# Modulation sums split around the low parts, their first product on ScalarE, and six loads moved to GpSimd's queue

## The chip, the cores and the metric

The program runs on one core of a Trainium2 chip. The metric is device time in microseconds (us), from the start of the program to its end on that core; lower is better. A core has TensorE (PE, matrix products), VectorE (DVE), ScalarE (ACT), GpSimd (POOL) and SyncE (SP, which here only issues transfers). Each runs its own list of instructions in order, and semaphores tie the lists together. Any of SP, GpSimd and ScalarE can issue a DMA; an instruction that waits holds back whatever stands behind it on its engine.

## The reference, cut to what matters

Two blocks are computed for 512 tokens of width 1024. The change touches the first alone:

```python
mod = silu(c) @ w_ada + b_ada              # c: 1 x 1024, w_ada: 1024 x 3072
shift, scale, gate = split(mod, 3)
h = x * (1 + scale) + shift                # 512 x 1024
p = h @ w_in
out_a = gmlp(p[..., :1536])                # u * v * silu(gate), v normed and mixed over tokens
out_b = rwkv7(p[..., 1536:])               # a recurrence over tokens, group norm, bonus, gate
o = concat([out_a, out_b]) @ w_out
x = layer_norm(ALPHA * x + gate * o)
```

The second block is latent attention with an MLP, and an HGRN2 mixer with an MLP.

## The kernel before

**Precision.** Every large product is made of three: an operand is split into a high part (`wh`, `aH`, a cast by ScalarE) and a low part (`wl`, `aL`, a subtraction by VectorE), and high×high, high×low and low×high are added in PSUM.

**The modulation** is the first 75 us. `w_ada`'s shift and scale columns come in four groups `g` of 256 columns each. For a group, VectorE forms the running sum `acc` = Σ over q of w_ada[q]·silu(c)[q] over eight 128-row pieces (128x512 numbers each): one tensor_scalar for q = 0 (line 343, shown by its helper's line as L127) and seven scalar_tensor_tensor (L132). TensorE then sums `acc` over the partitions with four products against ones, eight instructions in the trace (`sums`, "sm<-ones,acc"), and VectorE adds the bias: "mod". With mod, ScalarE turns the transposed x (`turned_x`, "sm<-ident,xt") into `h`, casts it to `aH`, and writes the residual `res`; VectorE makes `aL`. Tiles named "ada" hold w_ada (each half of a group, four pieces, is one tile of a ring of five), "raw" rows of w_in and other weights. A group loads 2 MB of w_ada and 0.5 MB of x, an iteration of the loop below 0.375 MB of w_in.

**The loop over k** = 0..7 multiplies h's eight slices of 128 columns by the rows of w_in, eighteen 512-column products each, group g = k // 2. In each iteration, after four of them (the constant SB = 1), TensorE transposes the x of k+1; in odd iterations the sums over the next group follow there. `part(g+1, 0)`, the first half of the next running sum, stands at the end of an even iteration, and `part(g+1, 1)`, the second half, in the next odd one, ahead of `sums`. The order of the code is the order on the engines here, held by a context (`ordered`).

**Later**, `out_gate` (lines 922 to 932) uses the same `ada_acc` for eight pieces of gate, 128x128 numbers a piece ("ga"). `ugate` (line 688) loads a finished tile of the gMLP branch's mix ("mx") back from DRAM and multiplies it by gelu(u) ("gsh") and the gate ("gt", "gbn"). `inverse` (lines 777 to 798) solves 32x32 triangular systems in 31 steps on VectorE with tiles XT, TV and a temporary, and passes the result through DRAM (scT) to `Tst` and `TTb`. `merge` (line 812) multiplies GpSimd's M by Tst on TensorE ("mg"), adds a unit matrix on VectorE ("Psb", L122) and multiplies by TTb: the first step of a chain over eight chunks. `post` (line 889) is the group norm of the chain's output, once per 128 tokens, with its scale and shift from DRAM (G2D, B2D, lines 909 and 911). While VectorE inverts, TensorE is fed with products of other branches. Here a scheduler orders instructions by priority, so that an edit can change places of its neighbours too.

Of the kernel before, what the change touches and what calls it, by code (L numbers as in the profile page):

```python
# [14 lines left out]
AF = mybir.ActivationFunctionType  # L15
# [5 lines left out]
P = 128  # L21
T = 512
# [9 lines left out]
FULL = slice(0, T)  # L32
LATE = (0, 0, 0, 0, 0, 2, 1, 0)
POSTS = (3, 4, 5, 7)
SB = 1
MB = 1
BEGUN = 1
TT = ("sm", "sm", "mm", "mm")
# [22 lines left out]
class Kern:  # L61
# [238 lines left out]
    def block1(self):  # L300
        nc, I, tc = self.nc, self.I, self.tc
# [10 lines left out]
        sc = b([P, 8], "sc")  # L312
# [7 lines left out]
        bonD, G2D, B2D, mixD, oaD = (dt_(n) for n in ("bonD", "G2D", "B2D", "mixD", "oaD"))  # L320
# [18 lines left out]
        def ada_acc(acc, raw, steps, q0=0):  # L339

            for q in steps:
                if q == 0:
                    self.ts(acc, raw[:, q - q0], sc[:, q : q + 1])
                else:
                    self.stt(acc, raw[:, q - q0], sc[:, q : q + 1], acc, ALU.mult, ALU.add)

# [31 lines left out]
        def part(g, cur, q):  # L378
            ada_acc(cur[2], cur[1][q], range(4 * q, 4 * q + 4), 4 * q)
# [25 lines left out]
        with self.ordered():  # L405
            self.petoken = "start"
            cur = load(0)
            rv = wrows(0)
            pt = turned_x(0, cur[0])
            part(0, cur, 0)  # L410
            part(0, cur, 1)
            sums(0, cur)
            w_ = self.wsplit(rv, 1, 6 * P)
            modulated(0, pt)
            for k in range(8):
                wh, wl = w_
                g = k // 2
                if k < 7:
                    rv = wrows(k + 1)
                if k % 2 == 0 and k < 6:  # L420
                    nxt = load(g + 1)
                for f in loads[3 * k : 3 * k + 3]:
                    f()
                tok = [slice(tb * P, (tb + 1) * P) for tb in range(NB)]
                for tb in range(NB):
                    self.mm(psv[tb], hH[k][:, tok[tb]], wh[:, 0, :T], k == 0, False)
                    self.mm(psv[tb], hH[k][:, tok[tb]], wl[:, 0, :T], False, False)
                    if tb == SB and k < 7:
                        pt = turned_x(k + 1, (nxt if k % 2 else cur)[0])
                        if k % 2:  # L430
                            part(g + 1, nxt, 1)
                            sums(g + 1, nxt)
                            cur = nxt
                        w_ = self.wsplit(rv, 1, 6 * P)
                        modulated(k + 1, pt)
                        if k % 2 == 0 and k < 6:
                            part(g + 1, nxt, 0)
                oz = ((T, psw), (T + P, psk))
                for o, pz in oz:
                    self.mm(pz, wh[:, 0, o : o + P], hH[k], k == 0, False)  # L440
                    self.mm(pz, wl[:, 0, o : o + P], hH[k], False, False)
                for tb in range(NB):
                    self.mm(psv[tb], hL[k][:, tok[tb]], wh[:, 0, :T], False, k == 7)
                for o, pz in oz:
                    self.mm(pz, wh[:, 0, o : o + P], hL[k], False, k == 7)
            self.petoken = None
            for k in range(8):
                self.st(nc.gpsimd.dma_start(out=xaD[k], in_=xa[k]))
# [237 lines left out]
            yield from part_gemm(w_in, 3072 + i * P, evac)  # L686

        def ugate(j, pool):
            mx = self.tl(pool, [P, T], "mx", bufs=1)
            nc.sync.dma_start(out=mx, in_=mixD[j])  # L690

            def u_evac(ps):
                ug = self.tl(pool, [P, T], "gsh", bufs=2)
                self.act(ug, ps, AF.Gelu_apprx_tanh)
                self.tt(mx, mx, ug, ALU.mult)

            def g_evac(ps):
                t = self.tl(pool, [P, T], "gt", bufs=2)
                self.act(t, ps, AF.Tanh, scale=0.5)
                x = self.tl(pool, [P, T], "gbn", bufs=1)  # L700
                self.copy(x, ps)
                self.stt(t, t, 1.0, x, ALU.add, ALU.mult)
                self.stt(t, mx, 0.5, t, ALU.mult, ALU.mult)
                nc.sync.dma_start(out=oaD[j], in_=t)

            yield from part_gemm(w_in, j * P, u_evac)
            yield from part_gemm(w_in, 1024 + j * P, g_evac)
# [12 lines left out]
        g = [prep(p) for p in range(4)]  # L720
# [44 lines left out]
        rp = rx_.enter_context(self.pool("rw", 1))  # L765
# [1 line left out]

        Xs = self.tl(rp, [P, 32, 32], "XT")
        Tm = self.tl(rp, [P, 32, 32], "TV")
        tmp = self.tl(rp, [P, T], "tmp", bufs=1)  # L770
        Bt = [r([P, 4, P], f"Bt{i}") for i in range(2)]
        Kt = [r([P, 4, P], f"Kt{i}") for i in range(2)]
        Tst = [r([P, 4, RC], f"Tst{i}") for i in range(2)]
# [118 lines left out]
        def post(tb):  # L892
# [13 lines left out]
            ts_ = slice(tb * P, (tb + 1) * P)  # L906
            yield
            g2 = self.tl(rp, [P, 4, P], "gsh", bufs=2)
            nc.sync.dma_start(out=g2, in_=G2D[:, :, ts_].rearrange("i p t -> p i t"))
            b2 = self.tl(rp, [P, 4, P], "gbn", bufs=1)  # L910
            nc.sync.dma_start(out=b2, in_=B2D[:, :, ts_].rearrange("i p t -> p i t"))
            ps = self.ptl("mg")
            for p in range(4):
                self.turn(ps[:, p * P : (p + 1) * P], yc.rearrange("p h i -> p (h i)")[:, p * P : (p + 1) * P])
# [909 lines left out]
```

## Time and profile before

| | us |
|---|---|
| median of three runs | 1630.25 (1630.16 to 1633.17) |
| the profiled execution's own time | 1626.63 |
| its span | 1624.5 |
| TensorE busy | 1546.4 (95%) |
| VectorE busy | 918.4 (57%) |
| ScalarE busy | 721.0 (44%) |
| GpSimd busy | 250.6 (15%) |
| mean granted clock of TensorE | 0.984 |

The span is what the trace covers; the execution's own time has 2.1 us more around it. A busy share is over the whole span; what an engine waits for is read from a stretch of it. In the rows, L127 is tensor_scalar, L132 scalar_tensor_tensor, L122 tensor_tensor, L136 an activation, L139 a copy or cast, L142 a matrix product, L148 a transpose: each is the helper that issues all of its kind, so rows are told apart by their tiles ("out<-in"). A granted clock of 1.00 is 2.4 GHz on TensorE, 0.50 is 1.2 GHz.

### The profile page before, as it was taken

To read this page: it belongs to the slowest core of one execution; us is meant where nothing else is said; L and a number is where in the kernel's file an instruction comes from. 1 tells how busy PE (TensorE), PEld (TensorE's weight loads), DVE (VectorE), ACT (ScalarE), POOL (GpSimd) and SP (SyncE) were. 2 spreads that over 40 slices of the span, in tenths; PEclk is the share of its full clock that TensorE was granted. 3 is DMA by queue.
4 is the path that set the end of the run, shared out by engine and by line. 5 is a ranking of instruction groups with operands and counts; after the bars stand their busy time and mean duration, and the time that the engine had idled before them with its cause. 6 is when DMAs were issued, how large, how long until landed. Compare 5 with 4: busy or idle time off the path is not lost. (4 is left out here: it accounts for less than half of the span.)

```text
span 1624.5 us, 21815 instructions
## 1 busy us (share of the span) xinstructions
PE 1546.4 (95%) x8309; PEld 1308.3 (81%) x8309; DVE 918.4 (57%) x1617; ACT 721.0 (44%) x1313; POOL 250.6 (15%) x406
## 2 busy tenths in 40 slices
PE   5899979989999999999999999999999999999997
PEld 4677768779978889888888897888888888888886
DVE  4568685667667838434343438667754824343445
ACT  3345425654655646333232335656745623322231
POOL 3120201214410013000000024223323200000000
PEclk9899999999999999999999999999999999999999
DMA  9533455543223122433333322322223223241421
GB/s 309 155 103 95 81 164 143 154 124 111 53 72 85 40 78 66 130 96 96 93 91 104 91 80 86 103 72 68 67 60 104 92 78 116 64 119 65 121 86 52
DMA packets 262091, 161.15 MB, mean 99 GB/s; under 512 B 29537, under 2 KB 242644, under 8 KB 261988
## 3 DMA queue, kind: packets, MB, share of 16 engines
q1 hardware_dynamic: 260260, 156.55, 33.4%
q0 software_dynamic: 1584, 2.97, 0.5%
q8 instruction: 65, 1.06, 0.3%
q14 instruction: 38, 0.31, 0.1%
q10 hardware_dynamic: 144, 0.26, 0.0%
HBM read 146.90 MB, written 11.53 MB: 98 GB/s over the span
## 5 line engine op out<-in xcount | busy, mean ns | idle before, releaser
L122 DVE TENSOR_TENSOR wl<-raw,wh 128x1024 fp32r<-128x1024 f32 (+3 forms) x244 | 286.8, 1177 | 307.8 <-ACT wh L139 303.6
L139 ACT CAST wh<-raw 128x1024 fp32r<-128x1024 f32 (+3 forms) x244 | 242.5, 996 | 468.6 <-PE mm L142 363.2
L142 PE MATMUL mm<-bL,wh 128*128 128x512 f32 (+1 forms) x752 | 281.3, 377 | 1.2 <-DVE bL L132 1.2
L142 PE MATMUL mm<-bH,wl 128*128 128x512 f32 (+1 forms) x752 | 280.6, 376 | 0.0
L142 PE MATMUL mm<-bH,wh 128*128 128x512 f32 (+1 forms) x752 | 278.4, 377 | 0.5 <-ACT t L136 0.4
L142 PE MATMUL mm<-aH,wh 128*128 128x512 f32 (+1 forms) x656 | 239.4, 366 | 6.6 <-DVE res L132 2.8
L142 PE MATMUL mm<-aH,wl 128*128 128x512 f32 (+1 forms) x656 | 236.9, 362 | 1.1 <-DVE wl L122 1.0
L142 PE MATMUL mm<-aL,wh 128*128 128x512 f32 (+1 forms) x656 | 237.1, 363 | 0.0
L142 PEld LDWEIGHTS mm<-bL,wh 128*128 128x128 f32 x752 | 140.7, 188 | 30.4 <-DVE bL L132 2.3
L142 PEld LDWEIGHTS mm<-bH,wl 128*128 128x128 f32 x752 | 140.7, 188 | 28.0
L142 PEld LDWEIGHTS mm<-bH,wh 128*128 128x128 f32 x752 | 138.7, 188 | 28.9 <-ACT t L136 0.8
L142 PEld LDWEIGHTS mm<-aH,wh 128*128 128x128 f32 x656 | 125.1, 191 | 27.5 <-issue 4.9
L142 PEld LDWEIGHTS mm<-aH,wl 128*128 128x128 f32 x656 | 125.2, 191 | 20.2 <-DVE wl L122 1.7
L142 PEld LDWEIGHTS mm<-aL,wh 128*128 128x128 f32 x656 | 125.5, 191 | 17.9 <-issue 0.2
L142 PE MATMUL mm<-wh,aH 128*128 128x512 f32 x288 | 114.8, 401 | 1.7 <-ACT aH L139 1.7
L142 PE MATMUL mm<-wl,aH 128*128 128x512 f32 x288 | 114.0, 398 | 0.0
L142 PE MATMUL mm<-wh,aL 128*128 128x512 f32 x288 | 109.1, 395 | 0.0
L139 ACT CAST aH<-t 128x512 fp32r<-128x512 f32 (+1 forms) x74 | 41.1, 563 | 75.6 <-DVE t L122 75.5
L142 PEld LDWEIGHTS mm<-wh,aH 128*128 128x128 f32 x288 | 55.3, 192 | 13.1 <-ACT aH L139 1.8
L122 DVE TENSOR_TENSOR aL<-t,aH 128x512 fp32r<-128x512 f32 (+1 forms) x74 | 45.1, 618 | 36.5 <-ACT aH L139 36.5
L142 PEld LDWEIGHTS mm<-wh,aL 128*128 128x128 f32 x288 | 55.3, 192 | 12.0
L142 PEld LDWEIGHTS mm<-wl,aH 128*128 128x128 f32 x288 | 55.4, 192 | 11.2
(548 smaller groups left out, 2622.4 us busy)
## 6 DMA issues: line engine op xcount, KB each, us to landing
raw<-in_mlp_w_dram SPq DMA_DIRECT2D x128, 512.0 KB
raw<-in_hgrn_w_in_dram SPq DMA_DIRECT2D x32, 512.0 KB
raw<-in_w_in_dram SPq DMA_DIRECT2D x23, 512.0 KB
ada<-in_w_ada_dram SPq DMA_DIRECT2D x16, 512.0 KB
raw<-in_w_out_dram SPq DMA_DIRECT2D x10, 512.0 KB
raw<-in_w_ada_dram SPq DMA_DIRECT2D x8, 512.0 KB
raw<-in_mla_w_o_dram SPq DMA_DIRECT2D x8, 512.0 KB
raw<-in_hgrn_w_o_dram SPq DMA_DIRECT2D x8, 512.0 KB
```

What stands on the lines that cost most here:

```text
L122: self.st((eng or self.nc.vector).tensor_tensor(out=out, in0=a, in1=b, op=op))
L139: self.st(self.nc.scalar.copy(out=out, in_=in_))
L142: i = self.nc.tensor.matmul(out, l, r, start=start, stop=stop, **kw)
```

## The change

1. `ada_acc`'s first product is an activation on ScalarE (Copy with a scale per partition) instead of VectorE's tensor_scalar: four times in the modulation (128x512), eight times in `out_gate` (128x128).
2. In the loop, `part(g+1, 0)` stands at the start of an even iteration, ahead of the split of k+1's weights and of `modulated(k+1)`, and `part(g+1, 1)` at its end. The transposes for k+1 (and in odd iterations the sums) come after two products in even iterations and after eight in odd ones, instead of after four.
3. `ugate` loads mx by GpSimd's queue into two buffers (one before). The room is made by the inverse's temporary, which shares the buffer "us" with a tile of the chain.
4. `post` loads G2D and B2D by GpSimd's queue.

```diff
--- before.py
+++ after.py
@@ -32,7 +32,6 @@
 FULL = slice(0, T)
 LATE = (0, 0, 0, 0, 0, 2, 1, 0)
 POSTS = (3, 4, 5, 7)
-SB = 1
 MB = 1
 BEGUN = 1
 TT = ("sm", "sm", "mm", "mm")
@@ -340,7 +339,7 @@
 
             for q in steps:
                 if q == 0:
-                    self.ts(acc, raw[:, q - q0], sc[:, q : q + 1])
+                    self.act(acc, raw[:, q - q0], AF.Copy, scale=sc[:, q : q + 1])
                 else:
                     self.stt(acc, raw[:, q - q0], sc[:, q : q + 1], acc, ALU.mult, ALU.add)
 
@@ -422,19 +421,20 @@
                 for f in loads[3 * k : 3 * k + 3]:
                     f()
                 tok = [slice(tb * P, (tb + 1) * P) for tb in range(NB)]
+                if k % 2 == 0 and k < 6:
+                    part(g + 1, nxt, 0)
                 for tb in range(NB):
                     self.mm(psv[tb], hH[k][:, tok[tb]], wh[:, 0, :T], k == 0, False)
                     self.mm(psv[tb], hH[k][:, tok[tb]], wl[:, 0, :T], False, False)
-                    if tb == SB and k < 7:
+                    if tb == (0, 3)[k % 2] and k < 7:
                         pt = turned_x(k + 1, (nxt if k % 2 else cur)[0])
                         if k % 2:
-                            part(g + 1, nxt, 1)
                             sums(g + 1, nxt)
                             cur = nxt
                         w_ = self.wsplit(rv, 1, 6 * P)
                         modulated(k + 1, pt)
                         if k % 2 == 0 and k < 6:
-                            part(g + 1, nxt, 0)
+                            part(g + 1, nxt, 1)
                 oz = ((T, psw), (T + P, psk))
                 for o, pz in oz:
                     self.mm(pz, wh[:, 0, o : o + P], hH[k], k == 0, False)
@@ -686,8 +686,8 @@
             yield from part_gemm(w_in, 3072 + i * P, evac)
 
         def ugate(j, pool):
-            mx = self.tl(pool, [P, T], "mx", bufs=1)
-            nc.sync.dma_start(out=mx, in_=mixD[j])
+            mx = self.tl(pool, [P, T], "mx", bufs=2)
+            nc.gpsimd.dma_start(out=mx, in_=mixD[j])
 
             def u_evac(ps):
                 ug = self.tl(pool, [P, T], "gsh", bufs=2)
@@ -767,7 +767,7 @@
 
         Xs = self.tl(rp, [P, 32, 32], "XT")
         Tm = self.tl(rp, [P, 32, 32], "TV")
-        tmp = self.tl(rp, [P, T], "tmp", bufs=1)
+        tmp = self.tl(rp, [P, T], "us", bufs=1)
         Bt = [r([P, 4, P], f"Bt{i}") for i in range(2)]
         Kt = [r([P, 4, P], f"Kt{i}") for i in range(2)]
         Tst = [r([P, 4, RC], f"Tst{i}") for i in range(2)]
@@ -906,9 +906,9 @@
             ts_ = slice(tb * P, (tb + 1) * P)
             yield
             g2 = self.tl(rp, [P, 4, P], "gsh", bufs=2)
-            nc.sync.dma_start(out=g2, in_=G2D[:, :, ts_].rearrange("i p t -> p i t"))
+            nc.gpsimd.dma_start(out=g2, in_=G2D[:, :, ts_].rearrange("i p t -> p i t"))
             b2 = self.tl(rp, [P, 4, P], "gbn", bufs=1)
-            nc.sync.dma_start(out=b2, in_=B2D[:, :, ts_].rearrange("i p t -> p i t"))
+            nc.gpsimd.dma_start(out=b2, in_=B2D[:, :, ts_].rearrange("i p t -> p i t"))
             ps = self.ptl("mg")
             for p in range(4):
                 self.turn(ps[:, p * P : (p + 1) * P], yc.rearrange("p h i -> p (h i)")[:, p * P : (p + 1) * P])
```

One line less at the top makes the helpers' line numbers one smaller in the rows of after (L121 is tensor_tensor, L131 scalar_tensor_tensor, L126 tensor_scalar, L141 a product, L147 a transpose).

VectorE in the modulation, from the low part of k=0's weights (wl) to that of k=2's activations; acc_222 is group 1's running sum, ada_214 and ada_219 its two halves. Before:

```order
L122 TENSOR_TENSOR wl_202<-raw_178,wh_201 128x768
L122 TENSOR_TENSOR aL_130<-h_48_205,aH_122 128x512
L122 TENSOR_TENSOR wl_236<-raw_210,wh_235 128x768
L122 TENSOR_TENSOR aL_131<-h_57_239,aH_123 128x512
L127 TENSOR_SCALAR acc_222<-ada_214,sc 128x512
L132 SCALAR_TENSOR_TENSOR acc_222<-ada_214,sc,acc_222 128x512 x3
L132 SCALAR_TENSOR_TENSOR acc_222<-ada_219,sc,acc_222 128x512 x4
L122 TENSOR_TENSOR mod<-sm_282,bada_111 128x2x2
L122 TENSOR_TENSOR wl_289<-raw_262,wh_288 128x768
L122 TENSOR_TENSOR aL_132<-h_63_292,aH_124 128x512
```

After:

```order
L121 TENSOR_TENSOR wl_202<-raw_178,wh_201 128x768
L121 TENSOR_TENSOR aL_130<-h_48_205,aH_122 128x512
L131 SCALAR_TENSOR_TENSOR acc_222<-ada_214,sc,acc_222 128x512 x3
L121 TENSOR_TENSOR wl_238<-raw_210,wh_237 128x768
L121 TENSOR_TENSOR aL_131<-h_57_241,aH_123 128x512
L131 SCALAR_TENSOR_TENSOR acc_222<-ada_219,sc,acc_222 128x512 x4
L121 TENSOR_TENSOR mod<-sm_286,bada_111 128x2x2
L121 TENSOR_TENSOR wl_293<-raw_266,wh_292 128x768
L121 TENSOR_TENSOR aL_132<-h_63_296,aH_124 128x512
L131 SCALAR_TENSOR_TENSOR acc_323<-ada_315,sc,acc_323 128x512 x3
```

The four rows of group 1's sum stood together behind both low parts; now its first half stands between aL of k=0 and wl of k=1, its second half behind aL of k=1, the tensor_scalar is gone, and group 2's sum (acc_323) begins behind aL of k=2.

TensorE in the odd iteration k=1, from its third product. Before:

```order
L142 MATMUL mm_154<-wh_235,aH_123 128x512
L142 MATMUL mm_154<-wl_236,aH_123 128x512
L148 MATMUL sm_273<-ident,xt_217 128x128 x4
L142 MATMUL sm_282<-ones,acc_222 128x1 x4
L142 MATMUL mm_155<-wh_235,aH_123 128x512
L142 MATMUL mm_155<-wl_236,aH_123 128x512
L142 MATMUL mm_156<-wh_235,aH_123 128x512
L142 MATMUL mm_156<-wl_236,aH_123 128x512
```

After:

```order
L141 MATMUL mm_154<-wh_237,aH_123 128x512
L141 MATMUL mm_154<-wl_238,aH_123 128x512
L141 MATMUL mm_155<-wh_237,aH_123 128x512
L141 MATMUL mm_155<-wl_238,aH_123 128x512
L141 MATMUL mm_156<-wh_237,aH_123 128x512
L141 MATMUL mm_156<-wl_238,aH_123 128x512
L147 MATMUL sm_281<-ident,xt_217 128x128 x4
L141 MATMUL sm_286<-ones,acc_222 128x1 x4
L141 MATMUL sm_157<-aH_123,wh_237 128x512
```

The transposes (sm<-ident) and the sums (sm<-ones) of the next group moved four products down.

VectorE from the ga products at the end of the inverse to the first merge (Psb) and the next rows; gt_1910 is the last gate of `ugate`, mx_1843 the last mix tile, ga_334 and ga_336 two sums of `out_gate`. Before:

```order
L127 TENSOR_SCALAR ga_336_1996<-raw_1994,sc 128x128
L132 SCALAR_TENSOR_TENSOR ga_336_1996<-raw_1994,sc,ga_336_1996 128x128 x3
L122 TENSOR_TENSOR wl_2109<-raw_2106,wh_2108 128x1024
L132 SCALAR_TENSOR_TENSOR ga_336_1996<-raw_1994,sc,ga_336_1996 128x128 x4
L132 SCALAR_TENSOR_TENSOR gt_1910<-gt_1910,gbn_1912 128x512
L122 TENSOR_TENSOR mx_1843<-mx_1843,gsh_1876 128x512
L132 SCALAR_TENSOR_TENSOR gt_1910<-mx_1843,gt_1910 128x512
L122 TENSOR_TENSOR Psb_1959<-mg_1954,ist 128x256
```

After, from the copy that ends the inverse:

```order
L797 COPY XT_1488<-TV_1489 128x32x32
L131 SCALAR_TENSOR_TENSOR ga_334_1985<-raw_1983,sc,ga_334_1985 128x128 x2
L121 TENSOR_TENSOR wl_2109<-raw_2106,wh_2108 128x1024
L131 SCALAR_TENSOR_TENSOR ga_334_1985<-raw_1983,sc,ga_334_1985 128x128
L121 TENSOR_TENSOR mx_1843<-mx_1843,gsh_1876 128x512
L131 SCALAR_TENSOR_TENSOR ga_334_1985<-raw_1983,sc,ga_334_1985 128x128 x3
L131 SCALAR_TENSOR_TENSOR ga_336_1996<-raw_1994,sc,ga_336_1996 128x128 x6
L131 SCALAR_TENSOR_TENSOR gt_1910<-gt_1910,gbn_1912 128x512
L131 SCALAR_TENSOR_TENSOR ga_336_1996<-raw_1994,sc,ga_336_1996 128x128
L131 SCALAR_TENSOR_TENSOR gt_1910<-mx_1843,gt_1910 128x512
L121 TENSOR_TENSOR Psb_1959<-mg_1954,ist 128x256
```

The copy XT<-TV comes later in the list, with one weight split and two gates of `ugate` now ahead of it, and mx_1843's product five rows earlier against the gate that uses it. On GpSimd four loads of mx stand among the fills of TV and ahead of the second chunk's M, and eight loads of the norms' inputs among the tail's small operations. From the beginning of the second block on, both programs have the same lists.

## Rows read from the trace of the kernel before

**Rows 1.** Waits of TensorE in 0 to 80 us: total us, times, longest us.

```profile
PE sm L142 <- DVE acc L132: 15.0, 4, 5.2
```

**Rows 2.** Windows, k=2 and k=3: span, busy us (instructions), granted clock, DMA share, GB/s.

```profile
36.33:40.91 4.58, 4.58 (x23) 3.77 (x22) 1.52 (x3) 2.62 (x4) 0.54 (x1) 1.00 1.05 356
40.91:53.17 12.26, 8.58 (x32) 7.02 (x30) 7.61 (x11) 2.61 (x4) 0.54 (x1) 0.72 0.62 200
```

**Rows 3.** Timeline of TensorE, k=1 to k=6: start, us, instruction [idle before <-releaser].

```profile
26.66 0.40 PE L142 MATMUL mm<-wh,aH 128*128 128x512 f32 x1
...
30.56 1.02 PE L142 MATMUL sm<-ones,acc 128*128 128x1 f32 x8 [2.38 <-DVE acc L132]
...
41.83 0.60 PE L148 MATMUL sm<-ident,xt 128*128 128x128 f32 x4
46.10 1.83 PE L142 MATMUL sm<-ones,acc 128*128 128x1 f32 x8 [3.68 <-DVE acc L132]
47.80 0.77 PE L142 MATMUL mm<-wh,aH 128*128 128x512 f32 x1
...
70.12 0.39 PE L142 MATMUL mm<-wh,aH 128*128 128x512 f32 x1
```

**Rows 4.** Timeline of VectorE, group 2.

```profile
40.48 5.48 DVE L132 SCALAR_TENSOR_TENSOR acc<-ada,sc,acc 128x512 f32<-128x512 f32 x7
47.98 0.16 DVE L122 TENSOR_TENSOR mod<-sm,bada 128x4 f32<-128x4 f32 x1 [2.02 <-PE sm L142]
48.15 0.96 DVE L122 TENSOR_TENSOR wl<-raw,wh 128x768 fp32r<-128x768 f32 x1
49.63 0.69 DVE L122 TENSOR_TENSOR aL<-h,aH 128x512 fp32r<-128x512 f32 x1 [0.53 <-ACT aH L139]
```

**Rows 5.** Timeline of ScalarE beside it.

```profile
50.00 0.82 ACT L139 CAST wh<-raw 128x768 fp32r<-128x768 f32 x1
```

**Rows 6.** Tile gsh, product by a column: ns shortest/median/longest, first and last start us.

```profile
L136 ACT ACTIVATE gsh<-gt,pb x4: 722/722/722, 263.8 to 305.9; 128x512 f32<-128x512 f32 x4
```

**Rows 7.** Window of 4 us in k=1, as Rows 2.

```profile
28.00:32.00 4.00, 1.62 (x12) 1.42 (x11) 2.67 (x6) 0.18 (x1) 0.00 (x0) 0.97 1.08 368
```

**Rows 8.** Window around a short wait of TensorE, as Rows 2.

```profile
201.00:207.00 6.00, 5.05 (x23) 3.82 (x22) 5.79 (x12) 1.54 (x2) 0.00 (x0) 1.00 0.32 88
```

**Rows 9.** Tile xaD, written by GpSimd's queue in the modulation, as Rows 6.

```profile
L448 POOL DMA_DIRECT2D xaD<-res x8: 539/540/575, 20.1 to 73.9; - x8
...
DMA to landing us min/median/max: 2.3/3.6/6.5
```

**Rows 10.** Tile mx, its loads by SP's queue and its first use, as Rows 6.

```profile
L690 SPq DMA_DIRECT2D mx<-mixD x4: 423/428/634, 185.0 to 239.4; - x4
L122 DVE TENSOR_TENSOR mx<-mx,gsh x4: 684/691/693, 203.1 to 242.3; 128x512 f32<-128x512 f32 x4
```

**Rows 11.** Timeline of TensorE after the filling work.

```profile
235.03 1.07 PE L142 MATMUL mg<-Tst,M 128*128 128x64 f32 x8 [1.60 <-DMA Tst<-scT]
244.06 1.97 PE L142 MATMUL mg<-TTb,Psb 128*64 128x128 f32 x8 [7.96 <-DVE Psb L122]
```

**Rows 12.** Timeline of VectorE from the end of the inverse.

```profile
226.60 1.14 DVE L797 COPY XT<-TV 128x1024 f32<-128x1024 f32 x1
...
227.79 1.23 DVE L122 TENSOR_TENSOR wl<-raw,wh 128x1024 fp32r<-128x1024 f32 x1
...
242.26 0.69 DVE L122 TENSOR_TENSOR mx<-mx,gsh 128x512 f32<-128x512 f32 x1 [3.68 <-DMA mx<-mixD]
...
243.59 0.42 DVE L122 TENSOR_TENSOR Psb<-mg,ist 128x256 f32<-128x256 f32 x1
...
244.40 2.68 DVE L132 SCALAR_TENSOR_TENSOR ga<-raw,sc,ga 128x128 f32<-128x128 f32 x7
```

**Rows 13.** Waits of SP's queue, 190 to 420 us, as Rows 1.

```profile
SPq L911 <- DVE gsh L122: 22.0, 3, 14.6
```

**Rows 14.** Waits of TensorE, 180 to 420 us.

```profile
PE mm L142 <- DVE res L132: 2.8, 1, 2.8
```

## The prediction

> **What bounds the kernel now.** I read the waits of TensorE first, because by the table it is busy 95% of the span: a change pays only where TensorE stands still or runs at its lower clock. In the first 80 us it waits four times, 15.0 us in all, for VectorE's running sum [rows 1]. The windows then show what such a wait costs. The even iteration k=2 takes 4.58 us at a granted clock of 1.00; the odd one k=3, with the same eighteen products and four transposes, takes 12.26 us at 0.72 [rows 2]. The timeline splits it: four products and the transposes until 42.43, 3.68 us of waiting, 1.83 us of sums, and then fourteen products from 47.80 to 53.17, 5.37 us [rows 3]. Four products before the wait took 0.92 us (40.91 to 41.83), 0.23 each; the fourteen took 0.38 each, since the clock had fallen to its lower level (1.2 GHz) behind the wait. An odd iteration thus takes 7.7 us more, some 3 of them by the clock (14 times 0.15, and 0.8 in the sums).
>
> The wait is there because VectorE works the group as one chain: mod, wl, aL, wl, aL, and only then the whole sum, 0.48 us and 5.48 us for seven parts, 0.78 each [rows 4]. Before it, VectorE idles in front of each aL, since the ScalarE and TensorE steps it needs come late. From one mod to the next, 31.62 to 47.98, are 16.4 us [rows 3, 4], the first of them 1.06 after the start of the sums at 30.56.
>
> The second place is at the end of the inverse. TensorE has finished its filling work, waits for Tst until 235.03, and then 7.96 us for Psb [rows 11]. VectorE reaches Psb at 243.59 only because the mx product before it stood 3.68 us for a transfer, with other rows between [rows 12]. That mx load, the fourth, was issued at 239.4 [rows 10], when the single mx buffer was free.
>
> **The modulation.** I count from a mod, at M, by the offsets of group 2 (M = 47.98).
> - VectorE: wl at M+0.17 [rows 4], aL from M+1.65 to M+2.34.
> - ScalarE: h, aH and res until M+2.02, where before the cast of the next weights began [rows 5]. The moved product stands there now. No row shows it on ScalarE; the nearest is a product by a column of the same size, 0.72 us [rows 6], so it ends at M+2.74 and the cast (0.82) at M+3.56. If it took 1.0, a period grows by 0.3.
> - VectorE: three parts of the sum from M+2.74 (2.35 us) to 5.09; wl 0.96 to 6.05; aL, 0.6 to the next start, to 6.65; four parts, 3.13, to M+9.8.
> - TensorE: sums at once, mod 1.06 later at the full clock: the period is 10.9 us.
> - TensorE's own work in it: ten products of the odd iteration left (2.3), an even iteration (4.58), eight products (1.84) and transposes (0.44): 9.2 us. It waits some 0.7 us per group, where it waited 3.7.
>
> Does the clock stay up over this? Around 202 us TensorE stood 0.95 us in a stretch of 6 us (5.05 busy), granted 1.00 throughout [rows 8]. I take it that it does; in the sums too TensorE has little to do, which is why the other answer is a rival.
>
> The first mod is where it was, since the first sum waits for its transfers. The start of k=1, at 26.66 [rows 3], isn't moved either: k=0 has the same products. Eight products and the transposes take it to 28.9, and mod(1) is at 29.9 where it was at 31.6. Two periods later mod(3) is at 51.7; ten products bring the start of k=6 to 54.0. It was at 70.12 [rows 3]. **Term: −16.1 us**, with bounds from −17.7 (TensorE's own 10.1 a period) to −7.7 (rival 1).
>
> The transfers can follow. Four groups of 2.5 MB and eight rows of 0.375 MB are 13 MB; at the 368 GB/s seen at full load [rows 7] that is 35 us, ended near 42, and the last group's second half is wanted at 47. The issues wait for weight buffers that VectorE frees earlier now. Moving the sums' transposes and the product leaves x's loads where they were.
>
> **The inverse and the first merge.** With two mx buffers the fourth load starts when the second tile is used up, instead of the third, and the inverse's rows hide it. Without the stall, VectorE's list counts. The order puts a weight split and two gates ahead of the copy XT<-TV, less one ga row: 1.23+0.69+0.69−0.28, some with overlap, 2.1 us [rows 12] (the split and a 128x512 row stand there). So the copy starts at 228.7 instead of 226.60. Then follow the copy (1.14), thirteen ga rows at 0.38 (2.68 for seven, rows 12: 5.0), a weight split (1.14 to the next start) and three 128x512 rows (0.6 to the next start): 9.0 us, and Psb at 237.7. Its other condition is Tst. It landed at 235.03 [rows 11]; the solution is 2.1 us later, but its four transfers now stand directly behind the stores, where a weight load and three TTb stood between. I take 235.3 (an estimate; 235.0 to 237.1 are the ends), and the 1.07 us product then ends before 237.7. TensorE goes on at 238.2 instead of 244.06. **Term: −5.9 us**; −3 if TTb or another late row holds it, −9 if the clock, which is low after the stand, rises sooner.
>
> What hides the moved ga products is ScalarE, idle for long stretches here; eight of 0.72 at most would be 5.8 us, of which I charge nothing. If that cover is gone, one product delays a ga row, and Psb stands behind thirteen of these: the −3 above holds it.
>
> **GpSimd's twelve issues.** An issue takes GpSimd 0.54 us, and a transfer issued there in the modulation landed after 2.3 to 6.5 us [rows 9]. SP is freed: line 911 held its queue for 22.0 us, once for 14.6 [rows 13], with weights of w_out behind it. Now that wait stands on GpSimd, ahead of the powers of the norm and the adds of the tail. TensorE's largest single wait in the tail is 2.8 us [rows 14], which bounds what freeing SP can give (−2.8); five issues in the tail on the path would cost 2.7, and a queue held for a whole wait another 1 to 2. **Term: +1 us** (two issues ahead of a power that the norm waits for), from −3 to +4.
>
> The Trainium skill speaks against this part. On the page "SBUF — State Buffer", section "SBUF: two separate sides", it says that descriptors of GpSimd's transfers are written through a port pair that VectorE can hold for a whole instruction, so that such a transfer starts late. By that rule each of the twelve could start up to one VectorE instruction late, here at most 1.23 us, 15 us if all lay on the path; the landings in rows 9, beside VectorE's sums, don't show more than 6.5 us, and the sum above stands without this rule.
>
> **Sum.** −16.1 −5.9 +1.0 = −21.0. From the profiled execution's 1626.63 us this gives 1605.6; the median shown lies 3.62 above that execution, so the forecast for the median is 1609.2 us. From 480 us on the lists are the same and shift as a block.
>
> **Rivals.**
> 1. *The clock still falls in each odd iteration* (0.13). For it: behind the 2.38 us wait in k=1 it fell as well. Against: the wait left is 0.7. Ten products at the low level cost 2.0 more, and the slower sums 0.8: three times 2.8 is 8.4, the modulation gives 7.7, and the time is 1617.6.
> 2. *The merge isn't earlier* (0.13): Psb's stall is replaced by Tst or TTb, late by the 2.1 us and the rearranged transfers. For it: TensorE already waited for Tst. Then −15.1 remains, 1615.1.
> 3. *The modulation doesn't shorten* (0.04), because VectorE or a late w_ada tile sets the same 16.4 us period and the edit doesn't do what it says; only the merge counts: 1625. Against: 7.6 us of VectorE's 12.26 in k=3 were busy [rows 2], and the DMA arithmetic above.
> 4. *Slower* (0.03): the mx loads on GpSimd come late. VectorE meets the first mx product in the middle of the inverse's rows, so a late mx holds the inverse, and with it the chain. The price counts from the slack: the first load was issued at 185.0 and its product on VectorE came at 203.1 [rows 10], 18 us later; with 21 us of gain elsewhere the kernel is slower when a load takes over 39 us, and at 45 it is 1636. Against: 6.5 us was the longest seen. The port rule of the page named above is the mechanism that would do it.
>
> **How the numbers follow.** The forecast has 0.67; its own range is 1604 to 1615. With rivals 1 and 2 most of the chance lies from 1601 to 1620. Under 0.2%, 3.3 us, a measurement of this kernel can't tell a change from none. Faster takes the forecast, rivals 1 and 2 and most of 3: 0.95; same 0.02; slower 0.03.
>
> **What would show it.** TensorE's waits for acc should fall from 15.0 to about 7 us (5.2 of it before k=0), the granted clock in k=3 and k=5 should be 1.00, and k=6 start near 54. Psb's wait should fall from 7.96 to about 2 us, and no wait for mx be left on VectorE. A clock of 0.7 in k=3, or a TensorE wait for Tst or TTb in place of Psb's, would prove the forecast wrong, and so would a GpSimd power or a weight load of the tail that TensorE waits for.

## The result: 1608.3 us, 22 us faster

| | before | changed |
|---|---|---|
| median of the runs beside each other, us | 1630.2 (1628.9 to 1633.2, 4 runs) | 1608.28 (1606.3 to 1612.1, 4 runs) |
| profiled execution, own time and span, us | 1626.63, 1624.5 | 1606.33, 1604.4 |
| mean granted clock | 0.984 | 0.990 |
| TensorE busy, us | 1546.4 (95%) | 1541.1 (96%) |

The ratio is 0.9866, 95% interval 0.9842 to 0.989. The forecast was 1609.2, range 1601 to 1620. A sum can come out right with wrong terms, so it is checked step by step here.

**The modulation.** TensorE's waits for VectorE's sum in the first 70 us (total, times, longest), where [rows 1] had 15.0:

```profile
PE sm L141 <- DVE acc L131: 6.3, 3, 5.2
```

5.2 of the 6.3 are the first wait, before k=0. The windows of k=2 and k=3, as in [rows 2]:

```profile
30.61:35.19 4.58, 4.58 (x23) 3.77 (x22) 4.09 (x7) 3.81 (x6) 1.09 (x2) 1.00 1.09 359
35.19:41.41 6.22, 5.68 (x31) 4.69 (x30) 4.37 (x7) 2.05 (x5) 0.00 (x0) 1.00 1.08 360
```

The odd iteration takes 6.22 us instead of 12.26, and the granted clock stays at 1.00. TensorE's timeline, against [rows 3]:

```profile
22.18 0.39 PE L141 MATMUL mm<-wl,aH 128*128 128x512 f32 x1
22.41 0.40 PE L141 MATMUL mm<-wh,aH 128*128 128x512 f32 x1
...
25.17 0.39 PE L141 MATMUL mm<-wh,aH 128*128 128x512 f32 x1
...
27.42 0.95 PE L141 MATMUL sm<-ones,acc 128*128 128x1 f32 x8
...
38.15 1.02 PE L141 MATMUL sm<-ones,acc 128*128 128x1 f32 x8 [0.54 <-DVE acc L131]
...
48.95 1.02 PE L141 MATMUL sm<-ones,acc 128*128 128x1 f32 x8 [0.56 <-DVE acc L131]
...
52.21 0.39 PE L141 MATMUL mm<-wh,aH 128*128 128x512 f32 x1
```

The sums of the first moved group (27.42) wait for nothing, the next two 0.54 and 0.56 us; k=6 starts at 52.21 instead of 70.12. VectorE over the same period, from mod to mod, against [rows 4]:

```profile
28.41 0.16 DVE L121 TENSOR_TENSOR mod<-sm,bada 128x4 f32<-128x4 f32 x1 [1.39 <-PE sm L141]
...
31.18 2.33 DVE L131 SCALAR_TENSOR_TENSOR acc<-ada,sc,acc 128x512 f32<-128x512 f32 x3 [0.42 <-ACT acc L135]
...
34.90 3.11 DVE L131 SCALAR_TENSOR_TENSOR acc<-ada,sc,acc 128x512 f32<-128x512 f32 x4
39.21 0.16 DVE L121 TENSOR_TENSOR mod<-sm,bada 128x4 f32<-128x4 f32 x1 [1.21 <-PE sm L141]
```

mod to mod is 10.80 us. Between the two halves of the sum stand wl and aL. ScalarE's product, which no row of before showed, takes 0.71 us:

```profile
30.44 0.71 ACT L135 ACTIVATE acc<-ada,sc 128x512 f32<-128x512 f32 x1
```

**The first merge.** VectorE from the copy that ends the inverse to Psb, against [rows 12]:

```profile
215.37 1.13 DVE L797 COPY XT<-TV 128x1024 f32<-128x1024 f32 x1
...
224.30 0.42 DVE L121 TENSOR_TENSOR Psb<-mg,ist 128x256 f32<-128x256 f32 x1
```

and TensorE, against [rows 11]:

```profile
222.76 1.00 PE L141 MATMUL mg<-Tst,M 128*128 128x64 f32 x8
224.78 1.09 PE L141 MATMUL mg<-TTb,Psb 128*64 128x128 f32 x8 [1.02 <-DVE Psb L121]
```

From the copy to TensorE's product with Psb are 9.4 us, where there were 17.5. VectorE waits for no mx tile any more; the loads on GpSimd's queue landed after 3.3 to 4.8 us, two of the four (issued at 193.6 and 203.4 us) in the middle of VectorE's inverse:

```profile
L690 POOL DMA_DIRECT2D mx<-mixD x4: 536/562/631, 160.1 to 203.4; - x4
...
DMA to landing us min/median/max: 3.3/4.1/4.8
```

The Trainium skill (page "SBUF — State Buffer", section "SBUF: two separate sides") says that GpSimd can't write the descriptors of its transfers while VectorE runs an instruction in a two-port mode; the prediction gave this rule without its condition. These landings are within those of [rows 9], and no run here shows such a hold. TensorE's waits from 160 to 410 us, against [rows 11, 14]:

```profile
PE mm L141 <- ACT gsh L135: 3.2, 1, 3.2
PE mm L141 <- ACT mla_cH L138: 2.7, 1, 2.7
...
PE mg L141 <- DVE Psb L121: 1.0, 1, 1.0
```

The wait for Psb is 1.0 instead of 7.96, that for VectorE's res does not come up any more, and a wait for ScalarE's gsh (3.2) is new.

**All runs by stages.** Every profile is cut at the same four places: the end of k=7 in the modulation, VectorE's first step of the inverse, its copy XT<-TV, and TensorE's first product with Psb. The first and last columns of us are times from the start; A to D are the stretches between the places and to the span's end.

| kernel | k=7 ends | A: to inverse | B: to copy | C: to merge | D: to end | span |
|---|---|---|---|---|---|---|
| before | 79.3 | 114.9 | 32.4 | 17.5 | 1380.4 | 1624.5 |
| changed | 61.3 | 118.6 | 35.5 | 9.4 | 1379.6 | 1604.4 |
| changed, again (e13) | 62.0 | 121.0 | 35.8 | 9.1 | 1381.2 | 1609.0 |
| e1: gate's products back | 62.0 | 118.7 | 33.8 | 11.4 | 1380.9 | 1606.8 |
| e6: norms' loads back | 62.1 | 119.7 | 35.8 | 9.5 | 1380.9 | 1608.0 |
| e8: mx on SP's queue | 61.9 | 113.7 | 35.2 | 10.0 | 1380.7 | 1601.5 |
| e11: modulation and mx | 61.7 | 117.7 | 33.8 | 10.5 | 1379.5 | 1603.2 |
| e2: modulation alone | 62.1 | 117.0 | 34.7 | 12.6 | 1384.3 | 1610.7 |
| e3: order of the loop alone | 63.8 | 117.5 | 34.7 | 12.9 | 1382.2 | 1611.0 |
| e7: ScalarE's products alone | 78.9 | 114.7 | 32.8 | 17.7 | 1382.4 | 1626.5 |
| e4: mx alone | 80.8 | 118.1 | 33.5 | 12.0 | 1382.9 | 1627.3 |
| e5: two mx buffers on SP | 80.9 | 117.1 | 32.1 | 17.8 | 1382.7 | 1630.6 |
| e9: norms' loads alone | 79.3 | 114.9 | 32.3 | 17.7 | 1382.9 | 1627.0 |
| e12: all but the modulation | 80.6 | 117.3 | 35.2 | 11.5 | 1390.1 | 1634.7 |

A profile is one execution, and those of one kernel scatter: e2's and e3's were their slowest (1612.5 and 1613.1 us, medians 1608.5 and 1611.6), e8's and e11's their fastest (1603.2 and 1604.9, medians 1606.2 and 1608.0). Verdicts are taken from the medians and ratios with the experiments. A ratio is to the runs of before beside it, with its 95% interval.

### The profile page after: what moved, and what is told of

It is laid out like the page before. It is cut to its first block, busy times and chain, and to the rows that moved or that the text cites. A ratio compares the mean times of both kernels' runs of the same rounds, so it can differ in the third digit from the quotient of the medians.

```text
span 1604.4 us, 21837 instructions
## 1 busy us (share of the span) xinstructions
PE 1541.1 (96%) x8309; PEld 1303.8 (81%) x8309; DVE 912.2 (57%) x1605; ACT 726.0 (45%) x1325; POOL 257.4 (16%) x418
## 5 line engine op out<-in xcount | busy, mean ns | idle before, releaser
L121 DVE TENSOR_TENSOR wl<-raw,wh 128x1024 fp32r<-128x1024 f32 (+3 forms) x244 | 286.5, 1175 | 304.8 <-ACT wh L138 300.6
L141 PE MATMUL mm<-bL,wh 128*128 128x512 f32 (+1 forms) x752 | 281.3, 377 | 1.2 <-DVE bL L131 1.2
L141 PE MATMUL mm<-bH,wl 128*128 128x512 f32 (+1 forms) x752 | 280.7, 376 | 0.0
L141 PE MATMUL mm<-bH,wh 128*128 128x512 f32 (+1 forms) x752 | 278.5, 378 | 0.3 <-ACT t L135 0.2
L141 PE MATMUL mm<-aH,wh 128*128 128x512 f32 (+1 forms) x656 | 240.2, 368 | 6.7 <-ACT gsh L135 3.2
L141 PE MATMUL mm<-aH,wl 128*128 128x512 f32 (+1 forms) x656 | 237.3, 363 | 0.8 <-DVE wl L121 0.8
L141 PE MATMUL mm<-aL,wh 128*128 128x512 f32 (+1 forms) x656 | 237.9, 364 | 0.0
L141 PEld LDWEIGHTS mm<-bL,wh 128*128 128x128 f32 x752 | 140.8, 188 | 30.1 <-DVE bL L131 2.4
L141 PEld LDWEIGHTS mm<-bH,wl 128*128 128x128 f32 x752 | 140.8, 188 | 28.0
L141 PEld LDWEIGHTS mm<-bH,wh 128*128 128x128 f32 x752 | 138.7, 188 | 28.8 <-ACT t L135 0.6
L141 PEld LDWEIGHTS mm<-aH,wh 128*128 128x128 f32 x656 | 125.3, 191 | 28.2 <-ACT gsh L135 3.6
L141 PEld LDWEIGHTS mm<-aH,wl 128*128 128x128 f32 x656 | 125.4, 191 | 20.0 <-DVE wl L121 1.0
L141 PEld LDWEIGHTS mm<-aL,wh 128*128 128x128 f32 x656 | 125.5, 191 | 18.2 <-issue 0.4
L141 PE MATMUL mm<-wh,aH 128*128 128x512 f32 x288 | 112.8, 394 | 1.7 <-ACT aH L138 1.7
L141 PE MATMUL mm<-wl,aH 128*128 128x512 f32 x288 | 112.2, 391 | 0.0
L141 PE MATMUL mm<-wh,aL 128*128 128x512 f32 x288 | 108.0, 390 | 0.0
L121 DVE TENSOR_TENSOR aL<-t,aH 128x512 fp32r<-128x512 f32 (+1 forms) x74 | 45.1, 617 | 36.5 <-ACT aH L138 36.5
L141 PEld LDWEIGHTS mm<-wh,aH 128*128 128x128 f32 x288 | 54.5, 189 | 13.0 <-ACT aH L138 1.8
L141 PEld LDWEIGHTS mm<-wl,aH 128*128 128x128 f32 x288 | 54.5, 189 | 11.0
L141 PEld LDWEIGHTS mm<-wh,aL 128*128 128x128 f32 x288 | 53.9, 188 | 11.4
```

The costliest lines, as they stand in the source:

```text
L121: self.st((eng or self.nc.vector).tensor_tensor(out=out, in0=a, in1=b, op=op))
L141: i = self.nc.tensor.matmul(out, l, r, start=start, stop=stop, **kw)
```

## The experiments

### The modulation and its two halves

**e2, the modulation alone**, and **e3, the order of the loop alone**, and **e7, the moved products alone.** e3 is, on the kernel before:

```diff
+                if k % 2 == 0 and k < 6:
+                    part(g + 1, nxt, 0)
                 for tb in range(NB):
...
-                    if tb == SB and k < 7:
+                    if tb == (0, 3)[k % 2] and k < 7:
...
-                            part(g + 1, nxt, 1)
                             sums(g + 1, nxt)
...
-                            part(g + 1, nxt, 0)
+                            part(g + 1, nxt, 1)
```

e7 has the product on ScalarE in the modulation, and VectorE's for the gate:

```diff
-                    self.ts(acc, raw[:, q - q0], sc[:, q : q + 1])
+                    (self.ts(acc, raw[:, q - q0], sc[:, q : q + 1]) if dve else self.act(acc, raw[:, q - q0], AF.Copy, scale=sc[:, q : q + 1]))
...
-            ada_acc(acc, raw, range(8))
+            ada_acc(acc, raw, range(8), dve=True)
```

e2 has both.

> The kernel before with the modulation's part alone: the order in the loop, and its first products on ScalarE. Gate sums, mx loads and the norms' loads as before. Theory: k=6 starts at 52.2 us as in the changed kernel (70.1 before), and the 17.9 us pass on to the end except for what the old stall at the first merge takes or gives: 1612, and the wait for Psb stays near 8 us. Rival: the longer stretch at the low clock at 146 to 162 us in the changed kernel belongs to the shifted work of that stretch and shows here too, and costs 5 us: 1617.

> The kernel before with the order of the loop alone; all first products stay on VectorE. Theory: the order makes the gain. VectorE is free for the first product at 2.3 us after mod, and ScalarE's product ended only at 2.7, so that the product on VectorE (0.48 us) ends at 2.8: a period of 10.8 us as with ScalarE, and k=6 at 52 to 53. Time as that of the modulation's part together, within 1.5 us. Rival: VectorE's 0.48 us comes on top in each group and k=6 starts at 54 or later.

> The kernel before with the modulation's first products on ScalarE and the order of the loop as before. Theory: the sums still stand behind both low parts; each group saves at most the 0.48 us of VectorE, the waits of TensorE for acc stay over 3 us and the clock falls after each: k=6 near 69 and 1629, not distinguishable from before. Rival: the moved product is what makes room: over 4 us less than before.

Measured: e2 1608.5 us, ratio 0.9876 (0.9861 to 0.9891); e3 1611.6, 0.9889 (0.9876 to 0.9903); e7 1628.4, 0.9998 (0.9988 to 1.0008). The modulation alone makes the whole gain that can be told, and its order makes it. e3 missed two numbers of its expectation: k=6 began at 54.66 us, which was the rival's sign, and its median is 3.1 us from e2's, not within 1.5.

```profile
54.66 0.39 PE L142 MATMUL mm<-wh,aH 128*128 128x512 f32 x1
```

The mods of e3 on VectorE:

```profile
30.79 0.16 DVE L122 TENSOR_TENSOR mod<-sm,bada 128x4 f32<-128x4 f32 x1 [2.14 <-PE sm L142]
...
41.61 0.16 DVE L122 TENSOR_TENSOR mod<-sm,bada 128x4 f32<-128x4 f32 x1 [1.21 <-PE sm L142]
...
52.43 0.16 DVE L122 TENSOR_TENSOR mod<-sm,bada 128x4 f32<-128x4 f32 x1 [1.21 <-PE sm L142]
```

They are 10.82 us apart, as with the product on ScalarE (10.80): the theory on the period holds, and the rival's 0.48 us in each group does not. k=7 ends 1.7 us later than in e2, of which 1.3 were there at the first sums (17.0 against 15.7 us), so the late k=6 and the 3.1 us between the medians are not shown to be the product's; the intervals of the ratios overlap. Without the order, the product buys nothing that can be told: TensorE waits for the sums as before (e7, first 60 us, three of the four waits):

```profile
PE sm L142 <- DVE acc L132: 11.1, 3, 5.2
```

e2 went against one part of its expectation. The wait for Psb, which was to stay near 8 us, was 0.5, though nothing of mx had been changed; what holds TensorE longer there is Tst, the condition that the prediction's rival 2 named:

```profile
224.40 1.53 PE L142 MATMUL mg<-Tst,M 128*128 128x64 f32 x8 [1.64 <-DMA Tst<-scT]
226.44 1.97 PE L142 MATMUL mg<-TTb,Psb 128*64 128x128 f32 x8 [0.52 <-DVE Psb L122]
```

The scheduler, working on the changed modulation, had put the fourth mx load ahead of the inverse's stores in SP's list (before it stood behind sixteen of Tst and TTb):

```profile
213.52 0.42 SPq L691 DMA_DIRECT2D mx<-mixD  x1
214.04 0.38 SPq L797 DMA_DIRECT2D scT<-TV  x1
```

So the stall of [rows 12] goes with one buffer too, when one row of SP's list stands elsewhere. The expectation's time (1612) is 3.5 us above the median, and its rival failed as well: the products that the inverse's inputs come from (AR with BK, near 150 us), which run at the low clock in the changed kernel (shown below), take 1.71 us for sixteen here. Stretch A is 2.1 us longer than before even so; TensorE's clock fell earlier in it (mean granted clock 0.80 from 125 to 142 us; before, 1.00 from 142 to 159).

### The mx part alone, and its queue

**e4** is the diff's hunks on `ugate` and on the inverse's temporary alone. **e5** is the same with `nc.sync` for the load. **e8** is the changed kernel with

```diff
-            nc.gpsimd.dma_start(out=mx, in_=mixD[j])
+            nc.sync.dma_start(out=mx, in_=mixD[j])
```

> The kernel before with the mx part alone: loads by GpSimd's queue into two buffers, the inverse's temporary in the chain's buffer. Theory A (the prediction's): the stall of VectorE for mx goes, Psb comes about 6 us earlier and the end with it: 1623. Theory B (from the modulation-only run, where the stall went without this part because the scheduler's order put the fourth load ahead of the inverse's stores): the same 6 us here, so that before's own stall is an accident of one row in SP's list: also 1623, but the modulation and this part don't add. Rival: the chain is held by Tst or later by the tail, and nothing comes out: 1629.

> As the mx part alone, but the loads stay on SP's queue: two buffers without the other queue. Theory: the second buffer is what matters; the fourth load is issued ahead of the inverse's stores and the wait for mx goes as with GpSimd's queue: the same time as that run within 1 us, about 1623. Rival: on SP the load that waits for its buffer holds Tst's loads behind it: 1629 or slower.

> The changed kernel with the mx loads back on SP's queue, two buffers kept. Theory: GpSimd's queue isn't what matters; the loads land in time on either and the time is 1607 to 1610. Rival: on SP a load that waits for its buffer holds the inverse's or the weights' transfers behind it, as with the two-buffer run on SP (Psb at 247.5 us, 3.9 later than before): 1612.

Measured: e4 1628.7, 0.9993 (0.9982 to 1.0004); e5 1632.3, 1.0011 (0.9999 to 1.0023); e8 1606.2, 0.9856 (0.9831 to 0.9882), which overlaps the changed kernel's interval. Both theories of e4 failed and its rival's time came, though not for the rival's reason (Tst or the tail). VectorE in e4:

```profile
198.95 0.19 DVE L122 TENSOR_TENSOR us<-XT,TV 128x31 f32<-128x31 f32 x1 [9.19 <-DMA XT<-scL]
...
232.41 1.12 DVE L797 COPY XT<-TV 128x1024 f32<-128x1024 f32 x1
...
243.97 0.42 DVE L122 TENSOR_TENSOR Psb<-mg,ist 128x256 f32<-128x256 f32 x1
```

Stretch C shortened by 5.4 us, of a kind with the prediction's 8; but the inverse began at 198.95 instead of 194.16 (1.6 of it already at the end of k=7, 3.2 in A) and took 1.0 longer. The merge came at 244.44, where it had been at 244.06. The 3.2 us are not TensorE's clock: its last eight products AR,BK began at 181.49 (179.77 before), and VectorE's first step stood 17.5 us behind that instead of 14.4, waiting for the transfers between (9.19 us for XT, 6.15 before). Why these took longer is open. Two mx buffers are not enough for it: e5 and e12 have 17.2 and 16.8 us here, but the changed kernel, e1 and e8 13.8 to 14.8. In e5 another row took the place of the mx wait ahead of Psb, a gate sum that waits for its w_ada transfer:

```profile
247.25 0.28 DVE L127 TENSOR_SCALAR ga<-raw,sc 128x128 f32<-128x128 f32 x1 [3.75 <-DMA raw<-in_w_ada_dram]
247.45 0.42 DVE L122 TENSOR_TENSOR Psb<-mg,ist 128x256 f32<-128x256 f32 x1
```

e8 shows no such hold. So which row of VectorE's list stands blocked ahead of Psb changes with the lists, and neither queue is shown to be better. For e5 the rival's time (1629 or slower) is the nearer, though it was a load of w_ada that was late, not one of Tst; for e8 it is the theory's (1607 to 1610, 0.8 above what came).

### The gate's products on ScalarE

**e1** is the changed kernel with `dve=True` for the gate, as in e7. **e12** is the changed kernel with the modulation's order and products of before: what is left of the change is the gate's products, mx and the norms' loads.

> The changed kernel with one part undone: the first products of the gate's sums (ga, 128x128) go back to VectorE; those of the modulation stay on ScalarE. Theory: in the changed kernel ScalarE, in order, stands 10.4 us at a ga product for its w_ada transfer, the gelu tile behind it comes late, and TensorE loses 3.2 us of waiting near 207 us and about 1.2 us at the lower clock after it. Without it that wait is gone and the time is about 1604 (4 us under 1608.3). Rival: the inverse on VectorE ends when it did, so that the 4 us come back as a wait for Psb; then 1608 within 1 us.

> The changed kernel with the modulation as before (order of the loop and its first products on VectorE): the gate's first products on ScalarE, mx and the norms' loads moved. Theory: these three parts are worth what the stall at the first merge was, about 6 us: 1623. If the modulation-only run already holds this gain (1608.5, as the changed kernel's 1608.3), the sum of both runs' gains is more than the whole's, and the stall is the part counted twice. Rival: the parts give nothing by themselves either: 1629.

Measured: e1 1607.8, 0.9867 (0.9854 to 0.9881); e12 1637.9, 1.0050 (1.0037 to 1.0064): slower. In the changed kernel ScalarE does stand 10.4 us at a gate product, and gsh behind it is late:

```profile
205.13 0.40 ACT L135 ACTIVATE ga<-raw,sc 128x128 f32<-128x128 f32 x1 [10.36 <-DMA raw<-in_w_ada_dram]
...
206.37 0.59 ACT L135 ACTIVATE gsh<-mm 128x512 f32<-128x512 f32 x1
```

Undoing it takes 1.4 of TensorE's 3.2 us of waiting for gsh away, and the wait for Psb grows from 1.0 to 3.7:

```profile
PE mg L141 <- DVE Psb L121: 3.7, 1, 3.7
PE mm L141 <- ACT gsh L135: 1.8, 1, 1.8
```

The rival of e1 was right: what is gained at gsh comes back as a wait for VectorE. In e12 the same hazard falls on the chain itself. ScalarE, in order, waits at a gate product, with the copies of Bt and Kt behind it,

```profile
252.07 0.40 ACT L136 ACTIVATE ga<-raw,sc 128x128 f32<-128x128 f32 x1 [4.96 <-DMA raw<-in_w_ada_dram]
...
253.11 0.75 ACT L139 COPY Kt<-mg 64x256 f32<-64x256 f32 x2
```

and TensorE stands for them:

```profile
253.91 2.07 PE L142 MATMUL ss<-TV,Kt 128*128 128x128 f32 x8 [5.53 <-ACT Kt L139]
```

Stretch D is 9.7 us longer than before (7.2 longer than in e9), and this wait of 5.5 is the largest part of it that the trace shows; in e4 it is 0.30 at the same place. The eight products behind it took 2.07 us (1.16 in e4), so a part of the rest is TensorE's lower clock. Both the theory (1623) and the rival (1629) failed. Without the modulation's part the rest of the change is a loss; with it, the same instructions cost nothing that can be told.

### The norms' loads, and the rest

**e9** is the kernel before with both loads of `post` on `nc.gpsimd`; **e6** the changed kernel with both on `nc.sync`; **e11** is e6 with the gate's products on VectorE as well.

> The kernel before with the norms' loads alone on GpSimd's queue. The prediction took +1 us for this (bounds -3 to +4). Theory: SP's queue, free of the 14.6 us wait, loads w_out earlier, and TensorE's waits of 2.8 us for res and 2.3 us for mla_cH in the tail stay: 1628 to 1630. Rival: w_out's earlier landing lets TensorE work ahead in the tail and takes up to 3 us: 1626.

> The changed kernel with one part undone: the norms' loads back on SP's queue. By the prediction's term (+1 for the part, -3 to +4) 1607; theory from the norms-only run (no difference from before): within 1.5 us of the changed kernel's 1608.3. Rival: SP's wait at line 911 returns ahead of w_out's loads, and TensorE waits for weights in the tail: 1611 or more.

> The modulation and the mx part alone: the changed kernel with the gate's first products on VectorE and the norms' loads on SP's queue. Theory: the modulation makes the whole gain, and the other parts cancel within what the runs can tell: 1607 to 1609, as the modulation alone (1608.5) and the whole (1608.3). Rival: without the gate's waits on ScalarE and the norms' loads on GpSimd the merge's earlier start is kept to the end: 1604 or less, faster than the changed kernel.

Measured: e9 1631.3, 1.0008 (0.9996 to 1.0020); e6 1609.7, 0.9881 (0.9859 to 0.9904); e11 1608.0, 0.9869 (0.9846 to 0.9893). None differs from its counterpart beyond the intervals. e6 and e11 came as their theories had it; e9's median is above its theory (1628 to 1630) and its rival (1626), with an interval that holds no difference. e9's stretch D (1382.9) is that of e4, e5 and e7 too. No run beats the changed kernel by more than can be told.

### The changed kernel again

> The changed kernel unaltered, for a second profile. In the first, 4 us of the modulation's 18 were lost between k=7 and the first step of the inverse, while TensorE ran at its low clock from 146 to 161 us with the products that the inverse's inputs come from. Theory A: that stretch belongs to this program (the order of waits and products before it): the second profile has it in the same place within a few us, and the inverse starts near 180 again. Theory B: it falls differently in each execution: it is elsewhere or shorter, the inverse starts 2 us or more away from 179.9, and this is part of the scatter of the runs (1606 to 1612).

Measured: 1607.9, 0.9866 (0.9845 to 0.9888). Each theory has half: the low clock lies in the same place, but the inverse starts at 183.0, 3.1 us later. Here are the products that the inverse's inputs come from (AR with BK), in TensorE's list, with the window of 142 to 162 us under each. Changed kernel:

```profile
144.68 1.77 PE L141 MATMUL sm<-AR,BK 64*128 64x128 f32 x8 [1.57 <-ACT res L138]
...
149.23 3.09 PE L141 MATMUL sm<-AR,BK 64*128 64x128 f32 x16
...
154.26 3.09 PE L141 MATMUL sm<-AR,BK 64*128 64x128 f32 x16
```

```profile
142.00:162.00 20.00, 18.43 (x74) 15.34 (x74) 12.70 (x21) 6.17 (x10) 8.69 (x15) 0.58 0.30 63
```

again (e13):

```profile
146.03 1.93 PE L141 MATMUL sm<-AR,BK 64*128 64x128 f32 x8 [1.56 <-ACT res L138]
...
150.75 3.09 PE L141 MATMUL sm<-AR,BK 64*128 64x128 f32 x16
...
155.78 3.09 PE L141 MATMUL sm<-AR,BK 64*128 64x128 f32 x16
```

```profile
142.00:162.00 20.00, 18.44 (x82) 15.50 (x81) 14.05 (x22) 5.27 (x9) 7.92 (x14) 0.61 0.23 56
```

and e8, whose list on TensorE is the same up to the merge, but for single rows that one trace or the other lacks:

```profile
145.35 1.51 PE L141 MATMUL sm<-AR,BK 64*128 64x128 f32 x8 [1.57 <-ACT res L138]
...
149.57 1.71 PE L141 MATMUL sm<-AR,BK 64*128 64x128 f32 x16
...
152.30 1.71 PE L141 MATMUL sm<-AR,BK 64*128 64x128 f32 x16
```

```profile
142.00:162.00 20.00, 17.49 (x117) 14.53 (x117) 17.50 (x27) 8.62 (x14) 8.00 (x15) 0.91 0.35 82
```

In the first two the clock stays at its lower level (1.2 GHz) after a wait of 1.6 us, and sixteen products take 3.09 us; in e8 the same wait is followed by sixteen products in 1.71. Before, the clock fell at this place too, after 2.5 us, and was back by the third row:

```profile
162.91 2.07 PE L142 MATMUL sm<-AR,BK 64*128 64x128 f32 x8 [2.51 <-ACT res L139]
...
167.78 1.96 PE L142 MATMUL sm<-AR,BK 64*128 64x128 f32 x16
...
170.75 1.71 PE L142 MATMUL sm<-AR,BK 64*128 64x128 f32 x16
```

From the eight products behind the wait to the last eight AR,BK are 21.0 us in both profiles with the low clock (in the changed kernel from 144.68 to 165.70), 15.4 in e8 and 16.9 before. Stretch A is 118.6 and 121.0 us, 113.7 and 114.9, and VectorE's first step of the inverse waits for transfers that come from these products. Of the 3.1 us by which e13's inverse is later, 1.4 are there at the last of these products; the rest is the transfers. e1's profile has the low clock in this place too (sixteen products in 3.09 us at 155.61). What lets the clock come back sooner in one execution is open.

## Why the prediction was right, and where it wasn't

| step | forecast, us | measured, us |
|---|---|---|
| modulation, to the end of k=7 | −16.1 | −18.0 |
| A: from there to the inverse | 0 | +3.7 (+6.1 in e13) |
| B: the inverse, to its copy | +2.1 | +3.1 |
| C: from the copy to the merge | −8.0 | −8.1 |
| D: the tail and the rest | +1.0 | −0.8 |
| sum | −21.0 | −20.1 (span) |

**The modulation** was right in mechanism and near in size. The period is 10.80 (forecast 10.9), the waits 0.55 (0.7), the clock stays up, so that rivals 1 and 3 are out. That the start of k=1 "isn't moved either" failed: it came at 25.17 instead of 26.66. 0.3 us of this were there at the first sums (15.46 against 15.80); the rest is the clock, since k=0's products step by 0.23 us from 22.18 on, where before the step was still 0.43 us at 24.2. These 1.5 us are most of the 1.9 by which the term was too small, and put it beyond its own bound of −17.7. Why the clock rose sooner in k=0 is not shown.

**The merge** was right where it was worked out: the copy to the product with Psb was to take 9.5 us and took 9.4; the two gates and the weight split ahead of the copy were to cost 2.1, and B grew by 3.1. Wrong was what the term left out. It counted from the copy's old time, "the copy starts at 228.7 instead of 226.60", moved by the modulation's gain: the 115 us between k=7 and the inverse as a rigid block. They grew by 3.7, by TensorE's low clock in the stretch above. Of the 5.0 us that B and C gained, 3.7 are so lost again in this profile and more than all in e13 (6.1). TensorE goes on with Psb 19.3 us earlier than before, 18.0 of them the modulation's: the term of −5.9 came to −1.3. So most of rival 2's result (the merge isn't earlier) came about, by another way than rival 2's: not by Tst or TTb, but upstream.

It was also wrong as a claim on the edit. The term was credited to the second mx buffer; e2 has the stall gone without it, by the scheduler's new order, and e4 has the buffer without any gain. The 15 to 18 us of the modulation (e3, e2 and the changed kernel at the end of k=7) are shown to be the modulation's; the 5 us of B and C are not shown to be mx's, since e2 has 2.6 of them without it.

**The tail** was within its bounds, but its sign can't be told: D is 1380.4 to 1382.7 us in before, e4, e5 and e7, whose norms' loads are the same. e6 and e9 leave the norms' loads at 1 to 1.5 us in the medians (for the loads on GpSimd in e6, against in e9), within the intervals.

**The sum** came within 0.9 us because errors cancelled: the modulation gave 1.9 us more than its term and D 1.8 more, while the merge gave 4.6 less. That it is so close is luck; that the modulation carries it is not.

**Rival 4** (a late mx load) didn't occur: 4.8 us was the longest landing of mx in the changed kernel's profile, 5.1 in e13. The thing to fear was beside it: the gate's product on ScalarE, for which the prediction charged nothing because ScalarE is "idle for long stretches here". Idle isn't the condition: the product stands in order ahead of gsh, Bt and Kt and waits for a transfer. In the changed kernel this fell into slack, in e12 on the path.

## What to carry to other kernels

Split a long accumulation on the engine that others wait for around the short pieces that feed them, and place the consumer so late in its own list that the other engine's list has reached the end of the sum: here the odd iteration lost 3.1 us of waiting and with it the clock's fall, 6.0 us in all. When an instruction is moved to an idle engine, ask what it waits for and what stands behind it, not how busy the engine is. Where a scheduler orders the lists, a removed stall must be credited by undoing each part alone: here the stall went with an edit that didn't touch it, and gains at one place were lost upstream at another.

## What the runs showed of the hardware

The same list on TensorE, after the same wait of 1.6 us, ran 20 us at a mean granted clock of 0.58 and 0.61 in two profiles and 0.91 in a third (e8); the inverse then began at 179.9, 183.0 and 175.6 us. This is not the whole of the runs' scatter of 1606 to 1612: the two profiles with the low clock are 4.6 us apart in span (1604.4 and 1609.0). An issue of mx took GpSimd 0.54 to 0.63 us (SP in before: 0.42 to 0.63), one of the norms' B2D 0.75 to 0.82 (SP: 0.36 to 0.45), and these transfers from GpSimd's queue landed in 3.1 to 5.4 us.
